# The expert stage of a two-block model: second-table rows fetched apart from their gates, a reordered list of jobs, and fewer branches

## The chip, the cores and the metric

The kernel runs on one core of one Trainium2 chip. TensorE (PE) multiplies matrices, VectorE (DVE), ScalarE (ACT) and GpSimd (POOL) work on tiles in the on-chip memory, and DMA queues move data; POOL also issues the gathers, whose row numbers are read from a tile. The metric is device time per execution in microseconds (us). Before the change it was 2997.37 us (median of 3 runs, 2997.36 to 3000.99).

## The reference

Two blocks run one after the other on 256 tokens of width 2048. The change is in the last stage, the expert layer of the second block, and in the norm behind it:

```
def _peer(xn, w_query, sub_keys, u_tab, v_tab):     # u_tab, v_tab: 16384 x 2048
    ...                       # 8 heads x 16 best of 16384 experts for each token
    gate = jax.nn.softmax(best, axis=-1)
    def blk(args):
        xb, eb, gb = args
        hid = jax.nn.gelu(jnp.einsum('pd,phkd->phk', xb, u_tab[eb]), approximate=False)
        return jnp.einsum('phk,phkd->pd', (gb * hid).astype(xb.dtype), v_tab[eb])
    ...
h = h + _peer(hn, ...)
return _rmsnorm(h, final_norm_g)
```

## The kernel before, in words

All data are fp32. A product is made of three matmuls on parts that have been split into a high and a low half (`split`, L175 to L177: ACT writes the high half, DVE the low one). The expert stage has two halves.

The **U stage** multiplies all 16384 rows of `u_tab` with all tokens, in 128 units of 128 experts (`mm_c`, L225 and L226, into `pu`). A unit's result goes through gelu (L1901 to L1903). For units 0 to 125 it is written to a table `WG` in DRAM (L1905), beside the gates. The last two units are "dense": their 256 rows of `v_tab` are loaded whole, and their gates are applied on the chip. In the background of the U stage, `sort` makes lists of the experts that any token of the first 128 (a=0) or of the second 128 (a=1) needs, and `cuts`, the list lengths, which `regs` loads into registers (L1774, L1775).

The **V stage** goes over jobs (a, n) of 128 listed experts. A job gathers its gate rows from `WG` (L1808, 256 KB for a=0 and 128 KB for a=1) and its rows of `v_tab` (L1810, 1 MB), both issued by POOL; DVE multiplies gate and gelu (`hm`, L1817); ACT and DVE split the rows into `vwh` and `vwl` and the gates into `hh` and `hlo`; and PE makes a *visit*: 12 matmuls of 128x512 (`mm`, L1836, three for each of four banks) into the sums `acc[t]` of the token half t. Jobs (0, n) with n below 44 are visited for both halves, those from 44 to 51 if the register says so, and later ones once. 80 jobs with a=0 and 36 with a=1 (n from 44) are built into the program; tc.If skips a load, a split or a visit whose list is shorter. A surplus branch (L1948) in front holds the jobs beyond 80; on this input it isn't entered.

`upto` sets how far each step runs ahead of the visits: gathers five jobs, the gate product two, the splits one. The order of the instructions on each engine is made from this by a scheduler; `tc.issue_after(self.lastmm)` ties a step to a matmul. Rows land in seven tiles used in turn, three `vraw` and four `h8`; the `h8` tiles hold the U stage's input X until its last unit. At the end `end(t)` adds the residual (L1964), squares (L1965), multiplies with the norm's weight on POOL (L1967), takes the root on POOL (L620), scales (L1972, L1974) and writes the output (L1973, L1975). L2035 is the closing drain of all engines.

Of the kernel before, what the change touches and what calls it, by code (L numbers as in the profile page):

```python
# [169 lines left out]
class Kern:  # L170
# [1509 lines left out]
    def peer(self, keep, M, mixR, g1):  # L1680
# [80 lines left out]
        NR, ND, NQ0, NB, NC, NM = 32, 2, 44, 52, 77, 80  # L1761
# [18 lines left out]
        def cond(r, a, n):  # L1780
            both, first, second = reg[r]
            if a:
                return None if NB <= n < NC else (both <= n) & (second > n)
            return None if n < NC else first > n

        def when(c):
            return ExitStack() if c is None else tc.If(c)

        def jobs(ns):
            return [(a, n) for n in ns for a in range(2) if (n >= NQ0 if a else n < 128)]  # L1790
# [9 lines left out]

        def gather(job):
# [3 lines left out]
            k = n - NQ0 if a else n  # L1805
            off = lambda b: bass.IndirectOffsetOnAxis(ap=idx[:, a, b, k:k + 1], axis=0)
            with when(cond("load", a, n)):
                gp.indirect_dma_start(out=g.rearrange("p a b t -> p (a b t)"), out_offset=None,  # L1808
                                      in_=wghalf if a else wgrows, in_offset=off(0))
                gp.indirect_dma_start(out=r, out_offset=None, in_=i["pv"], in_offset=off(1))  # L1810

        def gate(job):
            a, n = job
            h = hm[job] = vs.tile([128, 2 - a, 128], F32, name=f"hm{a}", bufs=2)
            g = wg.pop(job)
            with when(cond("split", a, n)):
                v.tensor_tensor(h, g[:, :, 0], g[:, :, 1], op=OP.mult)  # L1817
# [4 lines left out]

        def prep(job):
            a, n = job
            wh, wl, hh, hlo = vt[job] = tiles(a)
            r, h = raw.pop(job), hm.pop(job)
            with when(cond("split", a, n)):
                self.split(hh, hlo, h)
                self.split(wh, wl, r)

        def mm(w, t, k=0, start=False):
            wh, wl, hh, hlo = w
            for e in range(4):
                es = slice(e * 512, (e + 1) * 512)
                for n, (a, b) in enumerate(((hh, wh), (hh, wl), (hlo, wh))):
                    m = pe.matmul(acc[t][e], a[:, k], b[:, es], start=start and n == 0, stop=True, skip_group_check=True)  # L1836
            return m.ins

        def first(n):
            if n < NC:  # L1840
                self.lastmm = mm(vt[0, n], 0)
            elif n < 128:
                with tc.If(reg["pe"][1] > n):
                    mm(vt[0, n], 0)

        def second(n):
            w = {a: vt.pop((a, n)) for a, n in jobs([n])}
            both, _, end = reg["pe"]
            if 0 in w and 1 in w:
                with tc.If(both > n) as c:  # L1850
                    mm(w[0], 1, 1)
                with c.Else(), when(None if NB <= n < NC else end > n):
                    mm(w[1], 1)
            elif 0 in w:
                mm(w[0], 1, 1)
            else:
                with tc.If(end > n):
                    mm(w[1], 1)

        def run(ns, tail=0, end=None):  # L1860
            js = jobs(ns)
            at = {j: k for k, j in enumerate(js)}
            done = [0, 0, 0]

            def upto(k):
                with tc.issue_after(self.lastmm) if end else ExitStack():
                    for x, (f, ahead) in enumerate(((gather, 5), (gate, 2), (prep, 1))):
                        while done[x] < min(len(js), k + ahead):
                            f(js[done[x]])
                            done[x] += 1  # L1870

            upto(0)
            for n in ns[:len(ns) - tail]:
                for j in jobs([n]):
                    upto(at[j] + 1)
                first(n)
                second(n)
            last = ns[len(ns) - tail:]
            for n in last:
                for j in jobs([n]):  # L1880
                    upto(at[j] + 1)
                first(n)
            if end:
                end(0)
            for n in last:
# [153 lines left out]
```

## Time and profile before

| | |
|---|---|
| median of 3 runs | 2997.37 us |
| profiled execution, its time | 2999.24 us |
| profiled execution, its span | 2997.5 us |
| TensorE busy | 2842.1 us, 95% |
| VectorE, ScalarE, GpSimd busy | 66%, 47%, 20% |
| matmuls of the visits (L1836), three groups of 644 | 254.0, 250.5 and 225.3 us |
| gathers of gates (L1808), 107 | 175.6 us |

Times inside the trace count from the start of the span. The visits begin at some 2507 us. A stretch is read by the busy time of each engine in it; what an engine waited for is the last event before it went on.

### The profile page before, as it was taken

To read this page: it belongs to the slowest core of one execution; us is meant where nothing else is said; L and a number is where in the kernel's file an instruction comes from. 1 tells how busy PE (TensorE), PEld (TensorE's weight loads), DVE (VectorE), ACT (ScalarE), POOL (GpSimd) and SP (SyncE) were. 2 spreads that over 40 slices of the span, in tenths; PEclk is the share of its full clock that TensorE was granted. 3 is DMA by queue.
4 is the path that set the end of the run, shared out by engine and by line. 5 is a ranking of instruction groups with operands and counts; after the bars stand their busy time and mean duration, and the time that the engine had idled before them with its cause. 6 is when DMAs were issued, how large, how long until landed. Compare 5 with 4: busy or idle time off the path is not lost. (4 is left out here: it accounts for less than half of the span.)

```text
span 2997.5 us, 44270 instructions
## 1 busy us (share of the span) xinstructions
PE 2842.1 (95%) x17208; PEld 2492.6 (83%) x17212; DVE 1970.3 (66%) x2991; ACT 1415.3 (47%) x1934; POOL 611.2 (20%) x391
## 2 busy tenths in 40 slices
PE   7889899999999799998999999999989998999996
PEld 7888899988878699987878887888878886888884
DVE  8857644555566766448658898777768544777764
ACT  4365333444444557344444444444434443555553
POOL 4360300000000200013000111000000003888882
PEclk9789999999999899999999999999999998999998
DMA  4235554444456454322565556587875767888883
GB/s 172 71 113 172 173 213 161 156 144 138 155 177 217 142 189 141 113 78 99 190 203 181 173 190 222 176 223 223 222 200 185 213 210 268 299 308 317 315 312 149
DMA packets 232097, 569.52 MB, mean 190 GB/s; under 512 B 84257, under 2 KB 117921, under 8 KB 216002
## 3 DMA queue, kind: packets, MB, share of 16 engines
q1 hardware_dynamic: 173986, 411.46, 42.6%
q0 software_dynamic: 23040, 136.46, 12.6%
q10 hardware_dynamic: 34848, 18.62, 2.0%
q8 instruction: 140, 2.29, 0.3%
q14 instruction: 83, 0.68, 0.1%
HBM read 526.89 MB, written 39.59 MB: 189 GB/s over the span
## 5 line engine op out<-in xcount | busy, mean ns | idle before, releaser
L153 DVE TENSOR_TENSOR wl<-raw,wh 128x1024 fp32r<-128x1024 f32 x685 | 883.6, 1292 | 670.3 <-ACT wh L152 669.3
L152 ACT ACTIVATE wh<-raw 128x1024 fp32r<-128x1024 f32 x688 | 727.0, 1058 | 921.1 <-PE pu L225 220.5
L225 PE MATMUL pu<-h,wh 128*128 128x512 f32 x2048 | 735.8, 400 | 4.8 <-DVE qy L1730 2.9
L226 PE MATMUL pu<-h,wl 128*128 128x256 f32 x2048 | 575.5, 281 | 9.4 <-DVE wl L153 9.4
L225 PEld LDWEIGHTS pu<-h,wh 128*128 128x128 f32 x2048 | 386.8, 189 | 96.8 <-DVE w L1902 4.2
L226 PEld LDWEIGHTS pu<-h,wl 128*128 128x128 f32 x2048 | 387.4, 189 | 11.1 <-DVE wl L153 11.1
L241 PE MATMUL pz<-wh,t 128*128 128x512 f32 x1024 | 336.1, 400 | 0.0
L1808 POOL DMA_INDIRECT wg<-WG,idx x107 | 175.6, 1641 | 704.9 <-DVEq L1948 658.5
L1836 PE MATMUL acc<-vwl,hh 128*128 128x512 f32 x644 | 254.0, 394 | 11.9 <-DVE vwl L177 7.1
L1836 PE MATMUL acc<-vwh,hlo 128*128 128x512 f32 x644 | 250.5, 393 | 0.0
L1836 PE MATMUL acc<-vwh,hh 128*128 128x512 f32 x644 | 225.3, 394 | 14.7 <-ACT vwh L176 14.4
L241 PEld LDWEIGHTS pz<-wh,t 128*128 128x128 f32 x1024 | 192.6, 188 | 40.6 <-issue 1.0
L241 PE MATMUL pz<-wl,t 128*128 128x512 f32 x512 | 201.4, 393 | 1.6 <-DVE wl L153 1.4
L241 PE MATMUL pso<-wh,t 128*128 128x512 f32 x640 | 200.7, 393 | 0.4 <-DVE th L1008 0.4
L177 DVE TENSOR_TENSOR vwl<-h,vwh 128x2048 fp32r<-128x2048 f32 x61 | 139.8, 2292 | 39.6 <-ACT vwh L176 36.4
L1836 PEld LDWEIGHTS acc<-vwh,hh 128*128 128x128 f32 x644 | 122.3, 190 | 41.5 <-ACT vwh L176 14.8
L1836 PEld LDWEIGHTS acc<-vwl,hh 128*128 128x128 f32 x644 | 122.6, 190 | 39.2 <-DVE vwl L177 8.3
L1836 PEld LDWEIGHTS acc<-vwh,hlo 128*128 128x128 f32 x644 | 122.7, 190 | 25.6
L241 PEld LDWEIGHTS pso<-wh,t 128*128 128x128 f32 x640 | 120.2, 188 | 26.8 <-DVE th L1008 0.8
L176 ACT ACTIVATE vwh<-h 128x2048 fp32r<-128x2048 f32 x61 | 116.6, 1912 | 48.3 <-DMA h<-pv,idx 47.6
L212 PE MATMUL pq<-t,wh 128*128 128x256 f32 x768 | 138.1, 283 | 0.0
L1903 ACT ACTIVATE w<-w 128x256 f32<-128x256 f32 x128 | 53.4, 417 | 173.0 <-DVE w L1902 173.0
(621 smaller groups left out, 5325.0 us busy)
## 6 DMA issues: line engine op xcount, KB each, us to landing
raw<-pu SPq DMA_DIRECT2D x256, 512.0 KB, 4.1
raw<-w_z SPq DMA_DIRECT2D x96, 512.0 KB, 3.3
raw<-w_fqi SPq DMA_DIRECT2D x48, 512.0 KB, 3.3
raw<-w_a_in SPq DMA_DIRECT2D x32, 512.0 KB, 3.3
raw<-w_q SPq DMA_DIRECT2D x32, 512.0 KB, 3.3
raw<-w_b_out SPq DMA_DIRECT2D x32, 512.0 KB, 3.9
raw<-w_conv SPq DMA_DIRECT2D x32, 512.0 KB, 3.6
raw<-w_gz SPq DMA_DIRECT2D x32, 512.0 KB, 3.3
```

The costliest lines, as they stand in the source:

```text
L152: self.nc.scalar.activation(h, t, AF.Copy)
L153: m = (engine or self.nc.vector).tensor_tensor(l, t, h.bitcast(F32), op=OP.subtract).ins
L176: self.nc.scalar.activation(h, x, AF.Copy)
L177: (engine or self.nc.vector).tensor_tensor(l, x, h.bitcast(F32), op=OP.subtract)
L212: mm = nc.tensor.matmul(ps, a[:, c], b(k), start=(k == 0 and n == 0), stop=(k == nk - 1 and n == len(ops) - 1))
L225: nc.tensor.matmul(ps, w[0][:, c], x[2](k), start=k == 0, stop=False, skip_group_check=True)
L226: mm = nc.tensor.matmul(ps[:, 0], w[1][:, c], x[0](k), start=False, stop=k == nk - 1, skip_group_check=True)
L241: self.nc.tensor.matmul(pss[tt], x[a](k)[:, ts], b[:, kk * 512:(kk + 1) * 512], start=(k == 0 and n == 0), stop=(k == nk - 1 and n == 2))
L1808: gp.indirect_dma_start(out=g.rearrange("p a b t -> p (a b t)"), out_offset=None, in_=wghalf if a else wgrows, in_offset=off(0))
L1836: m = pe.matmul(acc[t][e], a[:, k], b[:, es], start=start and n == 0, stop=True, skip_group_check=True)
L1903: act.activation(w1, w1, AF.Gelu)
```

## The change

V rows and gates become two steps, `gather` and `gather_gates`, with a look-ahead of five jobs each; the gate tiles move from pool `vr` to `vs`, and the dense units get a gate tile of their own, `gd`. The rows of jobs 0 to 4 are called for from U units 122 to 126, the rows of the jobs at places 0 and 2 of the order are split from units 124 and 125, and `upto(2, ..., [2, 3])` calls for the gate products of four jobs and the splits of three ahead of the surplus branch. That branch (now L1977) holds `spare`, another code for the surplus jobs with tiles of its own. All rows of n = 77 to 79 are loaded and split without a test; for n = 78 and 79 only PE tests whether to visit. POOL, ACT and DVE test only the jobs (1, n) with n from 44 to 51. In the order, n = 44 to 49 stand in the middle of the list, and four a=1 jobs at its end; `end(0)` comes ahead of these four. The output is written in eight pieces of 256 KB where it was four of 512 KB. PE loads seven registers where it was four.

```
-        NR, ND, NQ0, NB, NC, NM = 32, 2, 44, 52, 77, 80
+        NR, ND, NQ0, NB, NC, NM = 32, 2, 44, 52, 78, 80
...
-            for name, engines in (("pe", (ET.PE,)), ("split", (ET.Activation, ET.DVE)), ("load", (ET.Pool,))):
-                reg[name] = [nc.values_load(cuts[0:1, n:n + 1], engines=engines, min_val=0, max_val=256) for n in (0, 1, 3)]
-            reg["all"] = nc.values_load(cuts[0:1, 4:5], engines=(ET.PE, ET.Activation, ET.DVE, ET.Pool), min_val=0,
-                                        max_val=256)
...
+            for name, engines in (("pe", every[0:1]), ("split", every[1:3]), ("load", every[3:4])):
+                reg[name] = [load(n, engines) for n in ((0, 1, 3) if name == "pe" else (0,))]
+            reg["all"] = [load(n, every) for n in (0, 1, 3)]
+            reg["max"] = load(4, every)
...
+        def only(job, r):
+
+            return reg[r][0] <= job[1] if job[0] and job[1] < NB else None
+
         def gather(job):
-            a, n = job
             r = raw[job] = rawtile()
-            g = wg[job] = vr.tile([128, 2 - a, 2, 128], F32, name=f"wg{a}", bufs=4 - a)
...
-            with when(cond("load", a, n)):
-                gp.indirect_dma_start(out=g.rearrange("p a b t -> p (a b t)"), out_offset=None,
-                                      in_=wghalf if a else wgrows, in_offset=off(0))
-                gp.indirect_dma_start(out=r, out_offset=None, in_=i["pv"], in_offset=off(1))
+            with when(only(job, "load")):
+                fetch(r, i["pv"], place(job, 1))
+
+        def gather_gates(job):
+            a = job[0]
+            g = wg[job] = vs.tile([128, 2 - a, 2, 128], F32, name=f"wg{a}", bufs=4 - a)
+            with when(only(job, "load")):
+                gates(job, g)
...
+        def values(job):
+            wh, wl, hh, hlo = vt[job] = tiles(job[0])
+            with when(only(job, "split")):
+                self.split(wh, wl, raw.pop(job))
+
         def prep(job):
+            if job not in vt:
+                values(job)
+            with when(only(job, "split")):
+                self.split(vt[job][2], vt[job][3], hm.pop(job))
...
+        def visit(job):
             a, n = job
...
+            if NQ0 <= n < NB and a:
+                with tc.If(reg["pe"][0] > n) as c:
+                    mm(vt[0, n], 1, 1)
+                with c.Else():
+                    mm(w, 1)
+            elif n >= NC:
+                with tc.If(reg["pe"][1 + a] > n):
+                    mm(w, a)
             else:
...
+                self.lastmm = mm(w, a)
+                if n < NQ0:
+                    self.lastmm = mm(w, 1, 1)
...
-        order = sorted(range(NM), key=lambda n: (n + 0.5) / 50 if n < 50 else (n - 49.5) / (NM - 50))
+        both, single = [*range(25), *range(44, 50), *range(25, 44)], [*range(52, 66), 50, 51, *range(66, NM)]
+        order = sorted([((k + 0.5) / len(x), n) for x in (both, single) for k, n in enumerate(x)])
+        order = [(a, n) for _, n in order for a in range(2) if not a or n >= NQ0]
+        last = [j for j in order if j[0] and j[1] >= NB][-4:]
+        order = [j for j in order if j not in last] + last
+        done, ahead = [0] * 4, (5, 5, 2, 1)
+
+        def upto(k, after, stages=range(4), most=1 << 30):
+            with tc.issue_after(after):
+                for x in stages:
+                    while done[x] < min(len(order), k + ahead[x], most):
+                        (gather, gather_gates, gate, prep)[x](order[done[x]])
+                        done[x] += 1
...
-                g = vr.tile([128, 2, 2, 128], F32, name="wg0", bufs=4)[:, 0]
+                g = vs.tile([128, 2, 128], F32, name="gd", bufs=2)
...
+            if 121 < n < nn + 1:
+                upto(0, self.lastmm, [0], n - 121)
+            if n in (124, 125):
+                with tc.issue_after(self.lastmm):
+                    values(order[2 * (n - 124)])
+            if n == nn:
+                upto(0, self.lastmm, [1])
+
+        upto(2, self.lastmm, [2, 3])
...
-        with tc.If(reg["all"] > NM):
-            run(range(NM, NQ0 + 128))
+        with tc.If(reg["max"] > NM):
+            spare()
...
-            act.activation(x[0], x[0], AF.Copy, scale=r)
-            nc.sync.dma_start(o[:, 0:1024], x[0])
-            v.scalar_tensor_tensor(x[1], x[1], r, fg[1], op0=OP.mult, op1=OP.mult)
-            nc.sync.dma_start(o[:, 1024:], x[1])
-
-        run(order, 2, end)
+            for c in range(4):
+                x = hs[t][c % 2][:, c // 2 * 512:c // 2 * 512 + 512]
...
+                nc.sync.dma_start(self.out[t * 128:(t + 1) * 128, e:e + 512], x)
+
+        for k, job in enumerate(order):
+            upto(k + 1, self.lastmm)
+            if job == last[0]:
+                end(0)
+            visit(job)
+        end(1)
```

`place` gives the column of row numbers of a job, `fetch` issues a gather, and `gates(job, g)` fetches the gate rows into g.

On POOL, where its first V-stage gathers are issued: before, behind its register loads the surplus branch comes first, and the gathers follow behind it, gates and rows in turn.

```order
L1774 TENSOR_LOAD cuts_14375
L1774 ISA x2
L1775 TENSOR_LOAD cuts_14375
L1948 COMPARE_AND_BRANCH
...
L1948 UNCONDITIONAL_BRANCH
L1808 DMA wg0_29802<-WG_14376,idx_14374 128x512
L1810 DMA vraw_29801<-pv,idx_14374 128x2048
L1808 DMA wg0_29806<-WG_14376,idx_14374 128x512
L1810 DMA h8_29805<-pv,idx_14374 128x2048
```

The same place after the change (`vraw_23002` holds the rows of job 0, the next three `vraw` those of jobs 5 to 7, the four `h8` those of jobs 1 to 4; `wg0_23221`, `wg0_23223`, `wg1_23225` and `wg0_23227` are the gates of jobs 0 to 3).

```order
L1800 DMA vraw_23002<-pv,idx_14374 128x2048
L1800 DMA vraw_30288<-pv,idx_14374 128x2048
L1800 DMA vraw_30316<-pv,idx_14374 128x2048
L1800 DMA vraw_30332<-pv,idx_14374 128x2048
L1800 DMA wg0_23221<-WG_14376,idx_14374 128x512
L1800 DMA wg0_23223<-WG_14376,idx_14374 128x512
L1800 DMA h8_23054<-pv,idx_14374 128x2048
L1800 DMA h8_23106<-pv,idx_14374 128x2048
L1800 DMA h8_23162<-pv,idx_14374 128x2048
L1800 DMA h8_23219<-pv,idx_14374 128x2048
L1800 DMA wg1_23225<-WG_14376,idx_14374 128x256
L1800 DMA wg0_23227<-WG_14376,idx_14374 128x512
```

Twelve gathers now stand ahead of the branch, eight of rows and four of gates; the gates of jobs 4 to 7 stand behind it, and so do all later ones.

On DVE around the surplus branch, after the change (`vwl1_23165` belongs to job 2, `vwl0_23283` and `hlo0_23285` to job 1, `hm0_30336` to job 4; the branch's body is left out).

```order
L177 TENSOR_TENSOR vwl1_23165<-h8_23106,vwh1_23164 128x2048
L177 TENSOR_TENSOR vwl0_23283<-h8_23054,vwh0_23282 128x2048
L1774 TENSOR_LOAD cuts_14375 x4
L1977 COMPARE_AND_BRANCH
...
L1977 UNCONDITIONAL_BRANCH
L177 TENSOR_TENSOR hlo0_23285<-hm0_23274,hh0_23284 128x256
L177 TENSOR_TENSOR vwl1_30441<-vraw_30316,vwh1_30440 128x2048
L1826 TENSOR_TENSOR hm1_23276<-wg1_23225 128x128
L1826 TENSOR_TENSOR hm0_23278<-wg0_23227 128x256
L1826 TENSOR_TENSOR hm0_30336<-wg0_23229 128x256
L177 TENSOR_TENSOR hlo1_23167<-hm1_23276,hh1_23166 128x128
```

Before, no gate product or split of a listed job stood ahead of the branch. Now job 0 is whole ahead of it, job 1 lacks its `hlo`, and job 2's `hlo1_23167` stands behind the product of job 4's gates.

On POOL in the middle of the list, after the change: the tests of the a=1 gate loads with n from 44 to 51.

```order
L1800 DMA wg1_31692<-WG_14376,idx_14374 128x256
L1818 COMPARE_AND_BRANCH
L1800 DMA wg1_31783<-WG_14376,idx_14374 128x256
L1818 UNCONDITIONAL_BRANCH
L1818 ISA
L1818 UNCONDITIONAL_BRANCH
L1818 COMPARE_AND_BRANCH
L1800 DMA wg1_31875<-WG_14376,idx_14374 128x256
L1818 UNCONDITIONAL_BRANCH
L1818 ISA
L1818 UNCONDITIONAL_BRANCH
L1800 DMA h8_31716<-pv,idx_14374 128x2048
```

Before, such tests (L1807, one for gates and rows together) stood among the last jobs of the list; now there are two for each such job, with rows of unconditional jobs queued behind them.

## Rows read from the trace of the kernel before

**Rows 1.** busy time of each engine by stretch (columns in its first line)

```profile
core 0: us, PE busy (x) PEld busy (x) DVE busy (x) ACT busy (x) POOL busy (x), PEclk, DMA share, GB/s
...
2510.00:2520.00 10.00, 8.45 (x38) 6.66 (x36) 1.06 (x3) 0.42 (x1) 4.23 (x5) 1.00 0.37 120
2520.00:2530.00 10.00, 0.00 (x0) 0.00 (x0) 0.64 (x2) 1.21 (x2) 7.56 (x9) 0.66 1.01 383
2530.00:2540.00 10.00, 6.57 (x15) 4.69 (x16) 8.95 (x9) 7.25 (x6) 7.09 (x5) 0.50 1.01 411
2540.00:2550.00 10.00, 10.00 (x45) 8.31 (x44) 6.94 (x7) 6.09 (x6) 8.78 (x5) 0.99 0.87 297
2550.00:2900.00 350.00, 350.00 (x1545) 289.80 (x1545) 254.84 (x265) 193.69 (x176) 297.58 (x173) 1.00 0.87 313
...
2925.00:2950.00 25.00, 19.22 (x74) 15.68 (x75) 15.53 (x17) 9.90 (x10) 10.13 (x9) 0.86 0.72 269
2950.00:2975.00 25.00, 20.14 (x80) 15.51 (x78) 10.98 (x9) 7.89 (x7) 3.44 (x2) 0.93 0.16 54
2975.00:2997.50 22.50, 5.92 (x25) 4.43 (x24) 7.88 (x14) 7.42 (x18) 6.08 (x6) 0.70 0.23 93
```

**Rows 2.** PE in time, first visits: start, duration, what

```profile
2518.06 0.39 PE L1836 MATMUL acc<-vwh,hlo 128*128 128x512 f32 x1
```

**Rows 3.** waits of PE from 2515 us on: total, times, longest

```profile
PE acc L1836 <- ACT vwh L176: 14.4, 1, 14.4
```

**Rows 4.** the end, in time

```profile
2980.68 0.39 PE L1836 MATMUL acc<-vwh,hlo 128*128 128x512 f32 x1
...
2987.16 0.56 POOL L620 TENSOR_TENSOR ssf<-rs_a,mhalf 128x1 f32<-128x1 f32 x1 [1.65 <-DVE rs_a L618]
```

**Rows 5.** POOL's gate gathers, 2550 to 2900 us

```profile
L1808 POOL DMA_INDIRECT wg<-WG,idx x87 | 145.7, 1674 | 26.5 <-issue 22.9 <-DVE hm L1817 1.2 <-DMA h<-pv,idx 0.9
```

**Rows 6.** POOL in time, 2514 to 2546 us

```profile
2533.94 2.75 POOL L1808 DMA_INDIRECT wg<-WG,idx  x1 [2.00 <-DVE hm L1817]
...
2542.75 0.94 POOL L1810 DMA_INDIRECT h<-pv,idx  x1 [0.30 <-issue]
```

**Rows 7.** DVE in time, 2505 to 2535 us

```profile
2533.59 2.29 DVE L177 TENSOR_TENSOR vwl<-vraw,vwh 128x2048 fp32r<-128x2048 f32 x1
```

**Rows 8.** the page's groups of instructions

```profile
L1808 POOL DMA_INDIRECT wg<-WG,idx x107 | 175.6, 1641 | 704.9 <-DVEq L1948 658.5
L1836 PE MATMUL acc<-vwl,hh 128*128 128x512 f32 x644 | 254.0, 394 | 11.9 <-DVE vwl L177 7.1
...
L176 ACT ACTIVATE vwh<-h 128x2048 fp32r<-128x2048 f32 x61 | 116.6, 1912 | 48.3 <-DMA h<-pv,idx 47.6
```

**Rows 9.** issues of DMAs, 2514 to 2545 us: KB, us to landing

```profile
wg<-WG,idx POOLq DMA_INDIRECT x10, 7.0
h<-pv,idx POOLq DMA_INDIRECT x5, 8.0
```

**Rows 10.** the surplus branch, ns min/median/max, first and last start

```profile
L1948 DVEq COMPARE_BRANCH  x1: 72/72/72, 2511.3 to 2511.3; - x1
...
L1948 DVEq EVENT_SEMAPHORE  x1: 21/21/21, 2514.2 to 2514.2; - x1
```

**Rows 11.** the tests of L1807 on POOL

```profile
L1807 POOLq INC_SWDGE_SEM  x9: 1991/2201/2326, 2897.7 to 2958.2; - x9
```

**Rows 12.** SP's transfers for the end, in time

```profile
2495.98 2.94 SPq L1956 DMA_DIRECT2D raw<-keep  x2
```

**Rows 13.** POOL's waits among the last jobs

```profile
POOL h L1810 <- DVE hm L1817: 7.7, 2, 7.4
POOL wg L1808 <- DVE hlo L177: 6.0, 1, 6.0
```

**Rows 14.** the closing drain

```profile
L2035 POOLq DRAIN  x3: 46/109/9515, 2987.1 to 2997.2; - x3
```

**Rows 15.** PE's register loads

```profile
L1774 PEldq TENSOR_LOAD <-cuts x3: 359/989/1149, 2202.1 to 2205.0; - x3
```

More of the change, by code (lines that the diff above doesn't have):

```diff
@@ L1821, in tiles @@
             return w + [vs.tile([128, 2 - a, 128], F32R, name=f"{x}{a}", bufs=3 - a) for x in ("hh", "hlo")]
+        def values(job):
+            wh, wl, hh, hlo = vt[job] = tiles(job[0])
+            with when(only(job, "split")):
+                self.split(wh, wl, raw.pop(job))
         def prep(job):
-            a, n = job
[L1825 to L1855, printed above, removed]
-            else:
[L1857 to L1885, printed above, removed]
-                second(n)
-            if end:
-                end(1)
@@ L1890, in peer, with mm @@
-        order = sorted(range(NM), key=lambda n: (n + 0.5) / 50 if n < 50 else (n - 49.5) / (NM - 50))
+            if job not in vt:
+                values(job)
+            with when(only(job, "split")):
+                self.split(vt[job][2], vt[job][3], hm.pop(job))
+        def mm(w, t, k=0, start=False, es=range(4)):
+            wh, wl, hh, hlo = w
+            for n, e in enumerate(es):
+                c = slice(n * 512, (n + 1) * 512)
+                for n, (a, b) in enumerate(((hh, wh), (hh, wl), (hlo, wh))):
+                    m = pe.matmul(acc[t][e], a[:, k], b[:, c], start=start and n == 0, stop=True, skip_group_check=True)
+            return m.ins
@@ new lines, in spare, with step @@
+        def spare():
+            block = lambda x, dt=F32R: [self.s.pool.tile([128, 1024], dt, tag=x, name=x, bufs=3) for _ in range(3)]
+            r, wh, wl = block("raw", F32), block("wh"), block("wl")
+            g = r[2][:, 0:512].rearrange("p (a b t) -> p a b t", a=2, b=2)
+            h, hh, hlo = [x[:, 512:768].rearrange("p (a t) -> p a t", a=2) for x in (r[2], wh[2], wl[2])]
+            at = vs.tile([128, 2], U32, name="sat")
+            halves = i["pv"].rearrange("r (c d) -> (r c) d", c=2)
+            def step(job, t, k=0):
+                gg, hk = (g[:, 0:1], h[:, 0:1]) if job[0] else (g, h)
+                gates(job, gg)
+                v.tensor_tensor(hk, gg[:, :, 0], gg[:, :, 1], op=OP.mult)
+                self.split(hh[:, 0:1] if job[0] else hh, hlo[:, 0:1] if job[0] else hlo, hk)
+                for c in range(2):
+                    v.tensor_scalar(at[:, c:c + 1], place(job, 1), 2, c, op0=OP.mult, op1=OP.add)
+                    fetch(r[c], halves, at[:, c:c + 1])
+                    self.split(wh[c], wl[c], r[c])
+                    mm((wh[c], wl[c], hh, hlo), t, k, es=(2 * c, 2 * c + 1))
+            both, once, end = reg["all"]
+            for n in range(NM, NQ0 + 128):
+                if n < 128:
+                    with tc.If(once > n):
+                        step((0, n), 0)
+                    with tc.If(both > n):
+                        step((0, n), 1, 1)
+                with tc.If((both <= n) & (end > n)):
+                    step((1, n), 1)
```

34 lines of the change are left out of this document (20 added, 14 removed).

## The prediction

> **What bounds the kernel now.** I read the busy time by stretch first. In the long middle of the visits PE is busy in all of its 350 us, so nothing there can be won except by fewer visits, and their number stays [rows 1]. 1545 matmuls in 350 us are 0.2265 us each, 2.72 us for a visit of twelve. PE stands still at both ends of the stage. [...] By 2550 PE has done 15 + 45 matmuls, five visits, worth 13.6 us; 2550 - 2518.45 is 31.55, so the start loses 17.95 us. At the other end, from 2925 to the last matmul's end at 2980.68 + 0.39 = 2981.07, there are 74 + 80 + 25 = 179 matmuls, worth 40.5 of 56.07 us: 15.5 us are lost [rows 1 and 4].
>
> The second engine to look at is POOL. In the middle it is busy 297.58 of 350 us in 173 gathers [rows 1], and each has some 0.30 us in front that is only issue [rows 6]: 297.6 + 51.9 makes 349.5, so POOL is as full as PE. It issues the gates of 87 jobs in 350 us, 4.02 us a job [rows 5]. A gather takes 0.94 us when it is alone, and 2.75 us where it starts beside DVE's split of 2.29 us, with its end 0.8 us behind that split's [rows 6 and 7]. ACT shows the same from its side: its splits waited 47.6 us for rows to land [rows 8]. There is no reserve behind PE, which decides most of what follows.
>
> [...]
>
> **The number of visits and loads.** 644 matmuls of one of three kinds, four to a visit, are 161 visits, 4 of them dense; 107 gate loads [rows 8] then mean 157 - 107 = 50 jobs visited twice, so (1, 44) to (1, 49) were skipped. 116 jobs are built, so 9 were skipped, the other 3 among n = 77 to 79. After the change those three are loaded and split as well: 110 loads, the same 161 visits.
>
> **The start.** By the order, twelve gathers stand ahead of the surplus branch. The rows of job 0 and of jobs 5 to 7 go into free `vraw` tiles and can land while U runs. The rows of jobs 1 to 4 go into `h8`, which hold X till the last unit, so they can't be issued before the last U matmuls, some 11 us (four visits) ahead of 2518.45, at 2507.3. With 8.0 us from issue to landing [rows 9] and 1 MB per 2.7 us at 383 GB/s they land at 2515.3, 2518.0, 2520.7 and 2523.4. So only job 0 is really ahead. Its two visits and job 1's one keep PE going from 2518.5 to 2526.6. Behind that I find two late things. DVE has job 1's `hlo` behind the branch, and that jump takes 2514.2 - 2511.3 = 2.9 us [rows 10]; this just fits or costs 1 us. Job 2's `hlo` stands behind the product of job 4's gates, and these are issued by POOL behind the branch, whose skip I take to wait for the landing of the earlier gathers: 2523.4 and 2.2 us for the skip [rows 11] make 2525.6, and 7.0 us for the gates to land [rows 9] 2532.6. PE would wait 6 us there. Together that is 7 us; bounds are 1 (gates land early and nothing waits) and 14 (the old gap, only moved). The 3 MB for the final norm, which SP loaded from 2496 on before [rows 12], come behind the branch now; at 400 GB/s they take 7.5 us from rows in a full stretch: 0 to 7, I take 2, since PE is already waiting for gates in part of that time. The start keeps 17.95 - 9 = 9 us of gain.
>
> [...]
>
> **The end of the list.** The tests no longer stand among the last jobs, so the 15.5 us go, if POOL keeps up. By PE alone the last matmul would end at 2981.07 - 17.95 - 15.5 + 9 = 2956.6.
>
> **What POOL can supply.** Before, the row gather of job 8 is issued at 2542.75 [rows 6]. After, POOL is through its branch at 2525.6, has four gates to issue (5 us) and can issue it at 2530.6. The last job that is visited, (1, 78), is a hundred loads later: 402 us, 2932.6. In between stand the tests of six skipped jobs, twelve since gates and rows are apart. Each ends in a semaphore instruction of 2.2 us [rows 11]. If that runs beside a waiting gather it costs as little as the 0.30 us of an issue, 3.6 in all; if POOL has to stand for it, 2.5 us, 30 in all. Before, these tests stood where POOL had time (10.13 of 25 us busy, [rows 1]); now they stand in the full middle, with rows of other jobs queued behind them. I take 1.2 each, between the two, 14.4 us: 2947. Landing 8.0, ACT's split 1.91, DVE's 2.29 and the visit 2.72 make 14.9 [rows 7 to 9]: the last visit would end at 2962, with 2951 to 2977.5 from the bounds. That is later than PE's 2956.6, so POOL decides.
>
> **The epilogue.** From the last matmul's end to the span's is 2997.5 - 2981.07 = 16.4 us; in it the closing drain of POOL runs 9.5 us, from about the second root at 2987.16 on [rows 4 and 14]. With `end(0)` done four visits earlier, half of the adds, squares and POOL's products are gone from there; I take 2 us, bounds 0 and 3.5. Eight writes for four I cost at nothing, since the drain runs beside them; if it waits for them, 1 us. The three more register loads on PE cost up to 1.1 us each [rows 15], in a stretch where it waits for DVE in part: 1 us, bounds 0 and 3.5.
>
> **Sum.** 2962 + 16.4 - 2 + 1 = 2977.4 of span; the profiled execution took 1.74 us more than its span, and the median is 1.87 below that execution: 2977, some 20 us or 0.7% faster. 0.2%, some 6 us, is about what a measurement of this kernel can tell from no change. From the last matmul to the median it is 15.3 us in each case below.
>
> **Rivals.**
> - *PE stays the bound.* The skips cost their 0.3 us and POOL speeds up wherever DVE pauses (0.94 against 2.75 us). Then 2956.6 + 15.3 = 2972, and 2964 if the start has no stall. For it speaks that PE had no idle time in the middle before; against it that POOL had none either. 0.25.
> - *POOL pays the full price.* Twelve skips at 2.5 us: 2977.5 + 15.3 = 2993, no change. For it: the middle is full. Against: before, nine of them went by partly beside gathers that waited anyway. 0.13.
> - *Slower: skips that also wait.* Among the last jobs POOL waited 6.0 and 7.4 us at loads beside such tests, for DVE's work on earlier jobs [rows 13]. If each of the six skipped jobs brings one 6 us wait on top, POOL is 36 us later: 3029; with three of them 3011. It decides from about three such waits on. Against it: the look-ahead is five jobs there, where the list's end has none. 0.10.
> - *The early rows aren't early.* Jobs 1 to 4 wait for X and for the branch as worked out, and if the split of job 1 is late as well, only job 0's 5.4 us are won, 4 less than in the sum, and POOL comes as much later: 2982. 0.07.
>
> The forecast itself has 0.45, with 2972 to 2986. Faster adds the forecast, the first and the last rival and a small part of the second: 0.79; within 0.2% 0.11; slower 0.10. The range of 8 in 10 runs from the first rival's lower value, some 2962, to behind the second, 2998.
>
> **What would show it.** After the dense visits PE goes on at once with job 0 and stands a few us before job 2 or 3; the granted clock stays high there. In the middle PE shows idle time against ACT or DVE, which wait for rows, most of it behind n = 44 to 49; POOL stays full there. From the last list visit to the end no wait is over 3 us, and the last matmul ends near 2962. The forecast is wrong if PE is full to the last visit (first rival), if POOL waits for semaphores in the middle (slower), or if the gap behind the dense visits stays over 10 us.

## The result and the profile after

The changed kernel takes 2977.97 us (median of 5 runs, 2973.22 to 2986.89), the kernel before 2997.45 us in the same comparison. The ratio is 0.9934, with a 95% interval of 0.9916 to 0.9952: 19.5 us or 0.65% faster. The forecast was 2977, with 2962 to 2998. The profiled execution of after took 2977.32 us, with a span of 2975.5 us. Single runs of the kernel before lie up to 17 us apart in these comparisons, so the parts below are read from the traces.

A measure for all of them: the *loss* at a visit is the time from the start of the first dense matmul to the start of this visit's last matmul, less 0.22655 us for each matmul between, which is PE's pace in the full middle of before. It grows only where PE stands or runs slowly. Worked out from the visits' matmuls, of one trace for each kernel (the four dense ones are visits 0 to 3; the experiments follow below):

| us | first U matmul | U stage | loss by visit 4 | 24 | 140 | 155 | 160 (last) | visits, in all | epilogue |
|---|---|---|---|---|---|---|---|---|---|
| before | 1674.95 | 832.4 | 17.9 | 18.7 | 18.9 | 34.6 | 35.8 | 473.7 | 16.4 |
| before_again | 1668.08 | 835.7 | 18.0 | 19.5 | 19.7 | 36.4 | 37.7 | 475.5 | 16.4 |
| after | 1669.16 | 835.0 | 4.0 | 10.6 | 13.8 | 15.3 | 21.7 | 459.8 | 11.6 |
| loads_mid | 1668.60 | 838.4 | 2.2 | 9.2 | 15.3 | 16.1 | 21.4 | 459.3 | 11.6 |
| end_late | 1669.42 | 835.7 | 3.5 | 12.0 | 14.4 | 18.2 | 24.1 | 462.0 | 11.6 |
| no_early | 1670.44 | 836.0 | 3.8 | 11.0 | 18.7 | 19.6 | 25.3 | 463.4 | 11.6 |
| end_pin | 1672.22 | 835.0 | 4.0 | 10.4 | 20.1 | 20.9 | 22.6 | 460.5 | 16.3 |
| loads_act | 1672.21 | 835.3 | 3.3 | 11.1 | 20.0 | 20.8 | 25.0 | 462.8 | 11.4 |
| shared | 1674.54 | 833.7 | 20.2 | 20.5 | 23.9 | 24.8 | 29.4 | 467.3 | 11.1 |
| before_spare | 1664.86 | 831.9 | 15.1 | 16.9 | 18.4 | 30.6 | 31.9 | 469.7 | 16.4 |
| old_order | 1671.81 | 837.9 | 15.3 | 17.1 | 26.0 | 26.5 | 35.8 | 473.7 | 11.1 |
| no_tests | 1671.13 | 837.0 | 2.4 | 10.1 | 30.4 | 32.2 | 38.7 | 476.8 | 11.1 |
| halves | 1672.35 | 836.6 | 3.9 | 4.7 | 4.8 | 5.6 | 8.9 | 446.7 | 13.9 |
| quarters | 1673.97 | 835.7 | 3.8 | 4.9 | 38.6 | 39.5 | 41.5 | 479.4 | 12.7 |

The two profiles differ by 22.0 us. Visits give 13.9 us of it and the epilogue 4.8 us. The rest, 5.8 us ahead of the U stage and 2.6 us back in it, is chance: the second trace of before has its first U matmul at 1668.08 us and a U stage of 835.7 us, like after. So the visits of after begin 3.2 us earlier in its trace than those of before, and that is no gain of the change.

Busy time by stretch of after, in the columns of [rows 1]:

```profile
2510.00:2520.00 10.00, 7.79 (x30) 6.10 (x29) 4.49 (x2) 7.73 (x5) 0.55 (x1) 0.87 0.62 249
...
2530.00:2540.00 10.00, 10.00 (x45) 8.07 (x44) 6.04 (x7) 2.43 (x3) 8.17 (x7) 1.00 1.03 414
2540.00:2550.00 10.00, 8.76 (x39) 6.95 (x38) 7.62 (x9) 8.45 (x8) 8.47 (x6) 1.00 1.01 413
2550.00:2700.00 150.00, 147.44 (x643) 121.31 (x642) 108.49 (x112) 78.07 (x72) 125.07 (x74) 0.99 0.87 316
2700.00:2750.00 50.00, 47.88 (x209) 38.68 (x208) 31.61 (x33) 25.95 (x24) 33.13 (x25) 1.00 0.72 259
2750.00:2900.00 150.00, 150.00 (x664) 124.24 (x663) 109.73 (x112) 81.62 (x74) 119.07 (x71) 1.00 0.85 307
...
2925.00:2950.00 25.00, 24.36 (x106) 19.28 (x105) 21.25 (x22) 16.11 (x17) 21.43 (x13) 1.00 0.91 347
2950.00:2975.50 25.50, 10.19 (x33) 7.13 (x31) 14.22 (x21) 10.46 (x20) 5.41 (x6) 0.72 0.24 89
```

The gap of 14.4 us behind the dense visits is gone, and the stretch from 2530 to 2540 is full. But from 2550 to 2700 PE is no longer full: 643 matmuls in 150 us are worth 145.7 us. In [rows 1] the whole middle was full. The last stretch has a granted clock of 0.72.

A stop cost more than its idle time where the clock fell behind it. At the visit that starts at 2576 PE stands 2.6 us and loses 4.8, since its next matmuls take 0.63 us each where the median of the visits' matmuls is 0.39. In loads_mid (an experiment below) it stands 1.9 us at the same visit and loses 2.4; the clock stays. Here are 2 us behind the stop in after, at a granted clock of 0.50, and 2 us behind that in loads_mid, at 1.00:

```profile
2580.00:2582.00 2.00, 2.00 (x7) 1.52 (x6) 2.00 (x1) 2.00 (x2) 1.70 (x2) 0.50 0.78 262
```

```profile
2583.00:2585.00 2.00, 2.00 (x10) 1.66 (x9) 2.00 (x1) 2.00 (x2) 1.70 (x2) 1.00 0.90 242
```

POOL's gathers in time (start, duration, idle before):

```profile
2292.15 1.15 POOL L1800 DMA_INDIRECT vraw<-pv,idx  x1 [441.78 <-DVE idx L1674]
...
2499.32 0.95 POOL L1800 DMA_INDIRECT wg<-WG,idx  x1 [192.68 <-PE pu L226]
...
2501.83 0.94 POOL L1800 DMA_INDIRECT h<-pv,idx  x1 [0.30 <-PE pu L226]
...
2508.17 0.95 POOL L1800 DMA_INDIRECT wg<-WG,idx  x1 [0.30 <-issue]
2519.45 0.94 POOL L1800 DMA_INDIRECT wg<-WG,idx  x1 [10.33 <-DMA h<-pv,idx]
...
2528.00 0.94 POOL L1800 DMA_INDIRECT h<-pv,idx  x1 [0.30 <-DVE hm L1826]
...
2546.00 2.89 POOL L1800 DMA_INDIRECT wg<-WG,idx  x1 [0.30 <-issue]
2549.19 2.81 POOL L1800 DMA_INDIRECT vraw<-pv,idx  x1 [0.30 <-DVE hm L1826]
...
2558.32 2.89 POOL L1800 DMA_INDIRECT wg<-WG,idx  x1 [0.30 <-issue]
```

Rows of job 0 go out at 2292, rows of jobs 1 to 4 from 2501.8, where before had its first gathers behind 2514. From 2546 to 2561 five gathers in a row take 2.7 to 2.9 us each, 14 us for what takes 0.94 us each when DVE is quiet. DVE's split beside the first of them:

```profile
2545.79 2.28 DVE L177 TENSOR_TENSOR vwl<-vraw,vwh 128x2048 fp32r<-128x2048 f32 x1
```

ACT then waits up to 12.7 us for a row, and PE for DVE's split; these are the waits in total, times, longest, of ACT (2545 to 2600) and of PE (from 2500 on):

```profile
ACT vwh L176 <- DMA h<-pv,idx: 14.5, 2, 12.7
```

```profile
PE acc L1848 <- DVE vwl L177: 7.2, 6, 2.4
PE acc L1848 <- PEq L1977: 2.2, 1, 2.2
```

The second wait is most of what is left of the gap behind the dense visits: PE is held by its own way past the surplus branch, whose compare-and-branch takes 6.3 us there, from 2511.1 on (3.7 us in before):

```profile
L1977 PEldq COMPARE_BRANCH  x1: 6259/6259/6259, 2511.1 to 2511.1; - x1
```

The tests in the middle, on POOL (ns min/median/max, first and last start), beside 2.2 us each in [rows 11]:

```profile
L1812 POOLq INC_SWDGE_SEM  x6: 380/578/787, 2728.9 to 2773.2; - x6
```

```profile
L1818 POOLq INC_SWDGE_SEM  x6: 527/1464/2300, 2691.6 to 2758.5; - x6
```

The end, all engines in time, and the closing drain, beside [rows 4 and 14]:

```profile
2945.51 0.29 DVE L1826 TENSOR_TENSOR hm<-wg 128x128 f32<-128x128 f32 x1
...
2947.69 4.15 POOL L1996 TENSOR_TENSOR raw<-raw 128x512 f32<-128x512 f32 x2
...
2949.31 1.38 DVE L1826 TENSOR_TENSOR hm<-wg 128x128 f32<-128x128 f32 x1
...
2950.61 1.38 DVE L177 TENSOR_TENSOR hlo<-hm,hh 128x128 fp32r<-128x128 f32 x1
...
2952.62 0.60 ACT L1994 ACTIVATE acc<-wh 128x512 f32<-128x512 f32 x1 [4.66 <-DVE wh L1993]
...
2954.07 1.90 ACT L176 ACTIVATE vwh<-h 128x2048 fp32r<-128x2048 f32 x1
...
2958.88 0.80 PE L1848 MATMUL acc<-vwl,hh 128*128 128x512 f32 x1 [2.37 <-DVE vwl L177]
...
2963.32 0.63 PE L1848 MATMUL acc<-vwh,hlo 128*128 128x512 f32 x1
```

```profile
L2072 POOLq DRAIN  x3: 112/193/1822, 2967.8 to 2975.1; - x3
```

The last visit runs at 0.63 us a matmul, behind a wait for its split; ahead of it POOL's products of `end(0)` (4.15 us for two) and DVE's small gate operations, 1.38 us where they take 0.29 us alone, stand beside each other. The rows aren't late there: those that ACT begins to split at 2954.07 were called for at 2938.90 and had landed at 2945.8. ACT's order has the squares of `end(0)` ahead of them, and these wait 4.66 us for DVE's add. The drain that lasted 9.5 us before is 1.8 us.

### The profile page after: what moved, and what is told of

It is laid out like the page before. It is cut to its first block, busy times and chain, and to the rows that moved or that the text cites. A ratio compares the mean times of both kernels' runs of the same rounds, so it can differ in the third digit from the quotient of the medians.

```text
span 2975.5 us, 44181 instructions
## 1 busy us (share of the span) xinstructions
PE 2839.9 (95%) x17212; PEld 2486.2 (84%) x17212; DVE 1984.1 (67%) x3002; ACT 1418.5 (48%) x1942; POOL 608.4 (20%) x397
## 5 line engine op out<-in xcount | busy, mean ns | idle before, releaser
L1848 PE MATMUL acc<-vwh,hh 128*128 128x512 f32 x644 | 249.4, 393 | 4.5 <-PEq L1977 2.2
L177 DVE TENSOR_TENSOR vwl<-h,vwh 128x2048 fp32r<-128x2048 f32 x64 | 146.3, 2289 | 27.8 <-ACT vwh L176 26.1
L1800 POOL DMA_INDIRECT vraw<-pv,idx x46 | 67.2, 1462 | 467.2 <-DVE idx L1674 441.8
```

The source lines that it names most:

```text
L177: (engine or self.nc.vector).tensor_tensor(l, x, h.bitcast(F32), op=OP.subtract)
L1800: gp.indirect_dma_start(out=out, out_offset=None, in_=table, in_offset=bass.IndirectOffsetOnAxis(ap=place, axis=0))
L1848: m = pe.matmul(acc[t][e], a[:, k], b[:, c], start=start and n == 0, stop=True, skip_group_check=True)
```

## The experiments

**loads_mid, end_late and no_early** tried to move steps by where they are called:

```
# loads_mid: hs and fg are loaded by a function that is called at place 70
+            if k == 70:
+                loads()
# end_late
-            if job == last[0]:
-                end(0)
             visit(job)
+        end(0)
         end(1)
# no_early: these lines go
-            if 121 < n < nn + 1:
-                upto(0, self.lastmm, [0], n - 121)
-            if n in (124, 125): ...  values(order[2 * (n - 124)])
-            if n == nn:
-                upto(0, self.lastmm, [1])
-        upto(2, self.lastmm, [2, 3])
```

> The changed kernel, with the 3 MB for the final norm (residual and weight) fetched in the middle of the list, at place 70 of the order, and no longer right behind the surplus branch. Theory A (these loads push the first rows back): the losses of PE between 2540 and 2590 us (1.7 us by visit 14, 4.8 us by visit 24) go, the stage from the first dense matmul to the last one takes 453 to 455 us where it took 459.8, and the time falls by 5 to 6.5 us, to about 2972. Theory B (POOL's issue is the limit, as the prediction had it): the stage shortens by less than 1.5 us. In both, the loads cost 0 to 1 us in the middle, where DMA is 72 to 82% busy.

> The changed kernel, with end(0) behind all visits, together with end(1). Theory A (end(0)'s work on DVE, ACT and POOL stands ahead of the last splits): the last visit's loss of 6.4 us falls below 1.5, the stage is about 5 us shorter, and the epilogue grows from 11.6 us back to 15 to 16.4; the time changes by less than 2 us. Theory B (the last rows are late from POOL): the last visit still loses some 6 us, the epilogue grows as in A, and the time rises by 4 us.

> The changed kernel without the early part: no rows, gates, values or products of listed jobs are called for ahead of the surplus branch. Theory A (the early rows won the start, at a price in the U stage): the loss by visit 4 goes from 4.05 us back to 15 to 18, PE's loss of 2.4 us between 2306 and 2320 us, beside the early gathers, is gone, and the time rises by 9 to 12 us. Theory B (the loss in the U stage has another cause): it stays, and the time rises by 12 to 14 us.

Measured: 2982.89, 2981.82 and 2983.29 us, ratios to before 0.9950 (0.9934 to 0.9966), 0.9944 (0.9927 to 0.9960) and 0.9949 (0.9934 to 0.9964). In all three the steps stand where they stood in after. SP's loads of loads_mid in time, and two of POOL's gathers of no_early:

```profile
2522.22 1.30 SPq L1987 DMA_DIRECT2D raw<-keep  x2
```

```profile
2294.13 1.15 POOL L1800 DMA_INDIRECT vraw<-pv,idx  x1 [442.49 <-DVE idx L1674]
...
2504.08 0.94 POOL L1800 DMA_INDIRECT h<-pv,idx  x1 [0.30 <-PE pu L226]
```

So loads_mid and end_late tested neither theory, and no_early says something else: without any early call the first rows go out at 2294 and 2504 us, and the loss by visit 4 is 3.8 us. The scheduler puts a step where its tiles are free. The early calls are not what made the early start.

Since the steps stand where they stood, the three are near repeats of after, and they show how far single traces can be trusted: the loss by visit 140 lies between 13.8 and 18.7 us in these four kernels, the visits between 459.3 and 463.4 us. A smaller difference between two traces is not read as an effect below. Their medians are 4 to 5 us above that of after, so the gain of the change is some 15 to 20 us rather than 19.5 to the digit.

**no_tests** loads and splits all jobs:

```
         def only(job, r):
-            return reg[r][0] <= job[1] if job[0] and job[1] < NB else None
+            return None
```

> The changed kernel with all jobs loaded, multiplied and split without a test on POOL, ACT and DVE: the six jobs (1, 44) to (1, 49) are fetched and split though no visit uses them; only PE tests. Theory A (POOL has a reserve in the middle): six more jobs of 4 us on POOL cost PE less than 4 us, and the 3.2 us lost at 2725 to 2745 us with the tests go; time within 3 us of the changed kernel's. Theory B (POOL's issue decides): the stage grows by 12 to 24 us, to 2990 to 3002.

Measured: 2998.66 us, ratio 0.9998 (0.9981 to 1.0014). The visits take 476.8 us, 17 more than in after, for six jobs that no visit uses. My theory A fell and B held: there is no reserve in the list. Which engine lacks it this run can't tell, since six jobs bring rows, splits and DMA time as well as gathers; halves, below, takes POOL apart. From 2750 to 2830 us, where these jobs come, PE does 293 matmuls, worth 66.4 of 80 us (columns as above):

```profile
2750.00:2830.00 80.00, 70.56 (x293) 54.86 (x292) 60.83 (x62) 41.90 (x39) 69.03 (x37) 0.98 0.81 291
```

**before_again** is the kernel before, unchanged.

> The kernel before once more, for its trace. The five profiles of changed kernels so far have the first matmul of the U stage 4 to 6 us earlier than the profile of before (1669 to 1671 against 1674.95 us), though the instructions up to there are the same. If that is chance, this profile has it within 1668 to 1673 us; if it belongs to the change, at 1674 to 1676 us. The stage of the visits should take 473 to 475 us again, the U stage 832 us and the epilogue 16.4 us.

Measured: 2997.46 us, one run; its trace is in the table. The lead ahead of the U stage was chance. So were the 2.6 us by which the U stage of after is longer, which I had put down to the early gathers: this trace has 835.7 us without any.

**before_spare** takes one part of the change alone, with the register loads that it needs:

```
         with tc.If(reg["all"] > NM):
-            run(range(NM, NQ0 + 128))
+            spare()
```

> The kernel before with one part of the change: the surplus branch holds the code spare(), with tiles of its own, and no longer run(), which uses the tiles of the listed jobs; nothing is called for early, and order, tests, gathers and writes stay. Theory C (the branch held the first gathers back because its body used their tiles; once it doesn't, the scheduler puts them ahead of it by itself): the loss by visit 4 falls from 17.9 us to 3 to 5 us, the 17 us lost among the last jobs and the epilogue of 16.4 us stay, the U stage is 2 to 4 us longer, and the time is 10 to 14 us below before. Theory D (the calls from U's last units make the early start): the loss by visit 4 stays over 15 us and the time within 3 us of before.

Measured: 2990.41 us, ratio 0.9983 (0.9966 to 1.0000). The gathers do go out early, but only 3 of the 14 us at the start are won. PE's longest wait there:

```profile
PE acc L1837 <- DVE w L1953: 10.8, 1, 10.8
```

It waits for `w`, the last U unit's own sum on DVE, which stands behind splits of listed jobs that wait for rows. The expectation had the gathers' place right and the loss by visit 4 (3 to 5 us) wrong.

**shared** is no_early with the branch's body on the listed jobs' tiles:

```
         def step(job, t, k=0):
+            r = [rawtile()[:, 0:1024] for _ in range(2)]
+            wh, wl, hh, hlo = tiles(job[0])
...          # the gates' tiles too; without tiles of its own from s.pool
```

> The changed kernel without the early calls (as the run no_early, whose first gathers still went out in the U stage) and with the body of the surplus branch on the tiles of the listed jobs, as before the change; all else as in no_early. Theory C (tiles in common with the branch's body hold the first gathers behind the branch): the first gather goes out at 2512 to 2516 us, the loss by visit 4 is 15 to 18 us where no_early has 3.8 us, and the time is 8 to 14 us above no_early's, 2991 to 2997 us. Theory D (other parts of the change make the early start): the loss by visit 4 stays below 6 us and the time within 3 us of no_early.

Measured: 2984.21 us, ratio 0.9952 (0.9939 to 0.9965). The first gather is at 2516 us again, and PE waits 17.9 us:

```profile
2516.05 1.15 POOL L1800 DMA_INDIRECT vraw<-pv,idx  x1 [658.93 <-DVEq L1970]
```

```profile
PE acc L1848 <- ACT hh L176: 17.9, 1, 17.9
```

The place of the gathers is as theory C has it: common tiles hold them behind the branch. The norm's loads show the same: SP issues them 11 us ahead of the first dense matmul in before and in shared, and 16 to 17 us behind it in no_early and in after, where the branch's body uses tiles of their pool. The time isn't as expected: the loss by visit 4 is 16 us larger than in no_early, yet the visits take only 3.9 us more, which is within the spread of the repeats, and the medians lie 0.9 us apart. From visit 4 to 155 it loses 4.6 us where no_early loses 15.8. That a later start finds more rows in store is my reading of this; no run here shows the store itself.

**old_order** puts the lists back in the order of their numbers:

```
-        both, single = [*range(25), *range(44, 50), *range(25, 44)], [*range(52, 66), 50, 51, *range(66, NM)]
+        both, single = [*range(50)], [*range(50, NM)]
```

> The changed kernel with the order of before: both lists in the order of their numbers, so that the tests of (1, 44) to (1, 51) stand among the last jobs again; n = 77 to 79 are still loaded without a test. Theory A (tests among the last jobs cost PE time): the losses behind visit 140 rise from 8 us to 14 to 20 us, the 3 us lost at 2725 to 2745 us go, and the stage takes 463 to 470 us where it took 459.8; time 2981 to 2988 us. Theory B (what cost time there were the tests for n = 77 to 79, gone in both): the losses behind visit 140 stay at 6 to 9 us, the stage at 456 to 461 us.

Measured: 2995.77 us, ratio 0.9993 (0.9976 to 1.0011), nearly all of the gain gone. Behind visit 140 it loses 9.8 us where after loses 7.9: between the theories, nearer to B. So by this trace the place of the tests of (1, 44) to (1, 51) explains little of the gain at the end of the list. The larger loss is at the start, where I had expected nothing: (1, 50), with its tests, is now the third job, and DVE's order has splits of listed jobs ahead of the last U unit's sum (L1923). DVE in time:

```profile
2520.06 2.29 DVE L177 TENSOR_TENSOR vwl<-h,vwh 128x2048 fp32r<-128x2048 f32 x1 [10.04 <-ACT vwh L176]
2522.27 2.28 DVE L177 TENSOR_TENSOR vwl<-vraw,vwh 128x2048 fp32r<-128x2048 f32 x1
2524.47 0.42 DVE L1923 TENSOR_TENSOR w<-w,pu 128x256 f32<-128x256 f32 x1
```

The first split waits 10 us for ACT, which waits 8.6 us for the rows, and PE stands 11.0 us for that sum, as in before_spare. In both kernels the third job carries a test; that the test is the reason for DVE's order wasn't tried by itself. A later loss of 6 us at some 2680 us begins with 1.9 us in which PE waits for DVE's split; its matmuls behind that take 0.63 us each.

**end_pin and loads_act** hold the two steps in place, by `tc.keep_in_program_order` on DVE's adds of end(0) and on loads issued by ACT:

```
# end_pin: end(0) behind the visits, as in end_late, and
                 m = v.tensor_tensor(o, o, acc[t][e], op=OP.add)
+                if t == 0:
+                    tc.keep_in_program_order(m)
# loads_act: at place 80
+                    tc.keep_in_program_order(nc.scalar.dma_start(hs[t][c], keep[t][:, cs]))
```

> The changed kernel with end(0) behind all visits, now with its first instructions on DVE held in the order of the code, behind the last products and splits of gates (in the run before, the scheduler put them where they had been). Theory A (end(0)'s work stands ahead of the last splits): the last visit's loss of 6.3 us falls below 2 us, the stage is 4 to 6 us shorter, the epilogue grows from 11.6 to 14 to 16.4 us, and the time changes by less than 2 us. Theory B (the last rows are late from POOL): the last visit still loses 5 to 6 us, the epilogue grows, and the time rises by 3 to 5 us.

> The changed kernel with the 3 MB for the final norm fetched on ACT's queue at place 80 of the order, held there in the order of the code (in the run before, the scheduler had left SP's loads behind the branch). Theory A (these loads push the first rows back): the 4 to 6.5 us lost between 2535 and 2590 us fall below 2.5 us and the stage takes 454 to 457 us. Theory B (these losses come from gathers that wait for DVE): they stay at 4 to 6.5 us and the stage at 459 to 462 us. In both, six issues on ACT cost up to 2 us near place 80.

Measured: 2983.50 us, ratio 0.9946 (0.9924 to 0.9969), and 2978.92 us, ratio 0.9942 (0.9924 to 0.9960). In end_pin the last five visits lose 1.7 us where after and its three near repeats lose 5.3 to 6.4, and the epilogue is 16.3 us: theory A holds for both, and moving `end(0)` ahead of four visits costs some 4 us there and brings 4.8. The eight writes are still in end_pin, so they brought nothing to the epilogue. Two losses of 4 us in the middle of its list hide this in its time; at each PE waits some 1.9 us for DVE's split, and its matmuls behind that take 0.57 us on average. In loads_act the 3 MB are issued at 2823 us:

```profile
2822.95 0.83 ACTq L1986 DMA_DIRECT2D raw<-keep  x2
```

The loss from visit 4 to 24 is 7.8 us, as in after (6.6): theory B. The loads behind the branch were not what cost PE there. Between visits 100 and 140, where they come now, it loses 3.3 us, a little over the 2 I had allowed.

**halves and quarters** cut DVE's split of the rows:

```
         def values(job):
...
-                self.split(wh, wl, raw.pop(job))
+                x = raw.pop(job)
+                act.activation(wh, x, AF.Copy)
+                for c in range(2):                       # quarters: range(4), 512 wide
+                    cs = slice(c * 1024, (c + 1) * 1024)
+                    v.tensor_tensor(wl[:, cs], x[:, cs], wh[:, cs].bitcast(F32), op=OP.subtract)
```

> The changed kernel with DVE's split of the rows in two instructions of 128x1024 where it was one of 128x2048. Theory A (POOL's gathers wait while DVE splits, and POOL's issue then sets PE's losses in the list): a gather takes 1.25 to 1.45 us on average in 2550 to 2700 us where it took 1.69 (125.07 us for 74), PE's losses between 2535 and 2945 us, some 11 us, fall by 5 to 9 us, the stage takes 451 to 455 us and the time is 2969 to 2974 us. Theory B (landing and DMA bandwidth set these losses): the gathers get shorter, the losses stay within 2 us. The second instruction costs DVE some 0.1 us a job, in its idle time.

> The changed kernel with DVE's split of the rows in four instructions of 128x512 (the run halves had two of 128x1024, the changed kernel one of 128x2048). Theory A (POOL's issue set PE's losses in the list, and with halves it no longer does): the gathers get shorter once more, from 1.29 to 1.1 to 1.2 us on average between 2550 and 2700 us, but the losses of PE behind visit 4, 5.0 us in halves, fall by 2 us at most; stage 444 to 447 us, time 2966 to 2971 us. Theory B (POOL is still the limit): the stage gets 3 to 5 us shorter. If the extra instructions make DVE the limit (some 0.1 us each, 0.2 us a job more than halves), the losses rise above 6 us.

Measured: halves 2970.68 us, ratio 0.9909 (0.9893 to 0.9925); quarters 2984.20 us (2968.74 to 3003.57), ratio 0.9962 (0.9944 to 0.9980). Halves from 2550 to 2700 us:

```profile
2550.00:2700.00 150.00, 149.58 (x660) 123.56 (x659) 118.61 (x161) 85.75 (x79) 100.32 (x78) 1.00 0.89 341
```

POOL needs 100.3 us for 78 gathers, 1.29 us each, where after needs 125.1 for 74. With 0.30 us of issue each that fills 147.3 of 150 us in after and 123.7 in halves: POOL was full, and now it has a reserve. The rows don't land sooner (8.2 us from issue to landing in the median, 7.9 in after), so landing isn't what changed, and up to visit 155 no visit of halves starts before both parts of its split are done, so PE doesn't gain by an early first part either. The loss behind visit 4 falls from 17.6 to 5.0 us. Of these 12.6 us, 2.3 come back in the epilogue, which is longer than that of after. It is the fastest of all kernels here, 7.3 us below the median of after and 11 to 13 below its near repeats; its interval overlaps a little with that of after, and with none of the three.

Quarters fits neither theory. Its loss behind visit 4 is 37.7 us, over the 6 us that I had named for DVE as the limit, but DVE isn't fuller than in halves (117 against 119 us from 2550 to 2700). The trace kept is that of the slowest of its 12 runs (3003.57 us); its fastest run took 2968.74 us, no more than halves. POOL and DVE of quarters in time:

```profile
2580.19 9.90 POOL L1800 DMA_INDIRECT vraw<-pv,idx  x1 [5.31 <-issue]
...
2625.56 10.23 POOL L1800 DMA_INDIRECT h<-pv,idx  x1 [2.95 <-issue]
...
2826.71 18.33 POOL L1800 DMA_INDIRECT h<-pv,idx  x1 [7.22 <-issue]
2845.34 0.95 POOL L1800 DMA_INDIRECT wg<-WG,idx  x1 [0.31 <-issue]
...
2880.18 18.32 POOL L1800 DMA_INDIRECT vraw<-pv,idx  x1 [7.34 <-DVE hm L1826]
```

```profile
2826.53 2.49 DVE L1839 TENSOR_TENSOR vwl<-h,vwh 128x512 fp32r<-128x512 f32 x4
2828.94 0.42 DVE L177 TENSOR_TENSOR hlo<-hm,hh 128x256 fp32r<-128x256 f32 x1
2829.28 0.28 DVE L1826 TENSOR_TENSOR hm<-wg 128x128 f32<-128x128 f32 x1
...
2841.53 2.49 DVE L1839 TENSOR_TENSOR vwl<-h,vwh 128x512 fp32r<-128x512 f32 x4
2843.94 0.28 DVE L177 TENSOR_TENSOR hlo<-hm,hh 128x128 fp32r<-128x128 f32 x1
```

Four gathers take 9.9 to 18.3 us. The third lasts from 2826.71 to 2845.04. DVE runs from 2826.53 without a gap to 2844.22, in short instructions, and the gather ends 0.8 us behind the last one. The other three end so too, 0.8 us behind the end of a row of DVE's instructions without a gap.

## Why the prediction was right, and where it wasn't

The sum was right to 1 us: 19.5 us faster where 20 was forecast. That it came so close is luck; that POOL and PE bound each other is not. By the traces, from the first dense matmul to the last one's end it took 459.8 us where the forecast had 454.6 (2962 less 2507.4), 5.2 more; the epilogue took 11.6 where 15.4 was forecast, 3.8 less; and the visits of after began 3.2 us earlier, by chance. So the last matmul ends at 2963.9, near the 2962 of the forecast, for a wrong reason. The terms by step:

- *Who decides.* "There is no reserve behind PE" and "POOL decides" held. no_tests shows the first (six more jobs cost 17 us), halves the second: shorter instructions of DVE take 12.6 us of loss away, with POOL's gathers shorter and the landing no faster. That POOL would keep the 4.02 us a job of before [rows 5] was my assumption; after issues the gates of 37 jobs from 2550 to 2700 us, 4.05 us a job. The first rival, PE as the bound, is out.
- *The start*, forecast at 9 of 18 us kept, counted from the last dense matmul's end, 2518.06 + 0.39 = 2518.45 [rows 2]. By visit 4 it is 14 us, by visit 24 8 us. The two delays I priced (job 2's gates, 6 us, and the norm's loads, 2 us) didn't come in that form. POOL did wait for the landing of the earlier rows, as forecast, but it was through the branch 15.2 us behind the first dense matmul where I had 18.2: the rows of jobs 1 to 4 went out from 2.4 us ahead of that matmul on, and the skip took 0.4 us where I had 2.2. I had X held to the last U matmul; its tiles come free one by one over the last unit. What PE met instead is its own way past the branch (2.2 us), which I hadn't priced. The rest of the loss is POOL's rate: PE starts 14 us earlier, DVE splits in bursts, and gathers of 2.7 to 2.9 us let rows be late by 2576.
- *What made the early start.* I gave it to the early calls. no_early shows that the start is as early without them; shared, that the branch's own tiles are needed; before_spare and old_order, that this isn't enough: in both the last U unit's sum is queued behind splits of the first jobs. That it takes first jobs without tests fits all these kernels and wasn't tried alone.
- *What it is worth.* shared against no_early: 16 us at the start are some 4 us at the end of the visits, by one trace each, and 1 us in the medians. The rest is given back in the list. The step on POOL had the principle, that the end of the list hangs on POOL's issues and not on PE's start, but it had no price for the give-back at its front.
- *The end of the list.* 15.5 us were to go. After visit 140 it was 16.9 us before, 7.9 after, of which some 4 are `end(0)`'s own, which I hadn't priced. The reason I gave, the place of the tests, isn't borne out: old_order has those of (1, 44) to (1, 51) among the last jobs again and loses 9.8 us there. What is seen is that POOL's gathers stood 6.0, 5.4 and 7.4 us there before, for DVE's work and an earlier landing ([rows 13] has two of them), up to 4.9 us in old_order, and no more than 0.3 us in after. Whether the tests of n = 77 to 79 or the gathers of rows and gates apart made the difference, no run separates; the cause of this largest part of the gain stays open.
- *The tests in the middle.* I took 14.4 us on POOL. The twelve of them take 12.2 us, 0.4 to 2.3 us each, and PE loses 3.0 us there (visits 76 to 82). Most of PE's loss in the list comes ahead of them, at visits 14 and 24, where I had expected it behind n = 44 to 49.
- *The epilogue.* Mis-sized: 4.8 us where 2 was taken, outside the bound of 3.5. end_pin shows that all of it is `end(0)`'s place. The drain isn't a fixed 9.5 us: in after it is 1.8 us.
- *The register loads*, taken at 1 us, show in no trace: the U stage is 835.0 us in after and 835.7 in the second trace of before.

So the time came out by terms that were off by 3 to 6 us each in both directions, round a bound that was right.

## What to carry to other kernels

When two engines are equally full, time won ahead of them can be mostly given back: here 16 us at the start came to some 4 at the end of the visits. Whether there is a reserve can be tested by adding a few jobs that do nothing. This scheduler issues by free tiles and not by the place of a call, so look at which tiles the body of a branch holds, even if it is never entered. An instruction that another engine's work waits out can be too long and too short: from 2550 to 2700 us a gather took 1.69 us on average with splits in one piece and 1.29 us with halves, and with quarters four gathers took 9.9 to 18.3 us. So its length has to be measured on both sides. And before a forecast that came out to the microsecond is called right, add up its terms against the trace.

## What the runs showed of the hardware

Most gathers that POOL started beside DVE's split of 128x2048 ended just behind it. In after POOL starts 215 gathers from 2500 to 2960 us, 101 of them while such a split of 2.29 us runs: 97 end 0.8 to 1.0 us behind the split's end, and the other four, which start within 0.04 us of the split's start, take 0.94 to 0.95 us. The 114 that start at other times take 0.93 to 1.18 us. The first of the five from 2546 on is one of the 97: it takes 2.89 us and ends 0.8 us behind DVE's split. I had not expected that shorter instructions could make it worse: in quarters four gathers stood for 9.9 to 18.3 us beside DVE's instructions back to back, while the gather of 2549.19 in after ends 0.8 us behind a split of 2.29 us, though DVE goes on without a gap. One trace shows the long ones, that of the slowest run; why these gathers didn't end between the short instructions wasn't tried.
